# Attention in a two-layer hybrid backbone: the value products of a pair of heads in one group, six buffers of transposed probabilities for four

## The chip, the cores and the metric

One core of a Trainium2 chip runs the whole program. The metric is the device time of one execution in microseconds (us); lower is better. TensorE is PE in the rows (its weight loads are PEld), VectorE is DVE, ScalarE is ACT, GpSimd is POOL, and SP issues the DMAs.

## What is computed

The reference is a backbone of two layers (DEPTH = 2) over 1024 latent and 256 context tokens, 1024 wide, in float32. A layer is a normalised input projection whose columns go to four mixers (mLSTM, differential attention, GLA, gated DeltaNet), a concatenation and an output projection. Only the attention is touched. It has 4 heads of width 64; each head has two maps of queries and keys of width 32:

```python
s = jnp.einsum('bhjqd,bhjkd->bhjqk', qblk, k).astype(F32) * scale
p = jax.nn.softmax(s, axis=-1)
wts = p[:, :, 0] - lam * p[:, :, 1]
return jnp.einsum('bhqk,bhkd->bhqd', wts.astype(v.dtype), v)
```

A block of 128 latent queries reads 1280 keys, a block of context queries 256. The second layer computes no context queries.

## The kernel before, in words

**How the order of the work is made.** The program is written as strands, Python functions that run as coroutines while the kernel is built. A planner (class `Issue`, line 141) keeps a modelled time for each engine and picks, for every instruction, the strand that can start earliest by that model; between strands that could start at the same time the lower rank goes first (`choose`, line 256). A strand whose instruction has waited over 3 us of modelled time (`patience`, line 143) goes ahead of all ranks. `need` stops a strand until another has issued the work of that name, `set` says that it was issued. On the chip each engine then runs its instructions in the order in which they were picked, with semaphores for the data.

**The strands of a layer.** The strand `left` (line 1180) does the input projection (rank 4, tile `mm`), then mLSTM, and asks for the end of the attention before mLSTM is opened (line 1189). The strand `right` (line 1200) does gated DeltaNet, then the attention, then GLA. So projection matmuls of rank 4 fill TensorE during the attention, and again during GLA until the projection is done.

**The attention (line 2276).** An item is one head and one block of 128 queries; a pair `m` is the two heads of one feature half for the same block, items 2m and 2m+1. There are 20 pairs in the first layer, 16 of them with 1280 keys (10 tiles of 128) and 4 with 256, and 16 pairs with 1280 keys in the second. The strands count cycles `c`, one item to a cycle:

- `on_pe` (line 2431, rank 0) issues the scores of item c: for map 0 two products of 512 columns into `sc0`, then both maps' 256 context keys into `sc2`, then map 1 into `sc1`. Each of these PSUM tiles has one buffer, so the next item's scores wait for the exponentials of this item.
- `on_dve` (line 2510, rank 0) takes the maxima, and one cycle later combines the two maps' probabilities in place (`p<-p,st,p`).
- `on_act` (line 2467, rank 0) takes the exponentials of each map, first of the 256 context keys, then of the 1024 latent keys. Between them it copies transposed probabilities from PSUM to SBUF (`turned`, line 2383, tile `wt`).
- `on_pe2` (line 2444, rank 1) transposes the combined probabilities (`turn`, line 2367, tile `tr`, one PSUM buffer), multiplies them with the values (`values`, line 2397, tile `po`, one PSUM buffer), and transposes the result back (`back`, line 2418).

The 10 key tiles of a pair are transposed in six steps k = 0 to 5: step k takes head k % 2 and the tiles 4(k // 2) onwards, so 4, 4, 4, 4, 2 and 2 tiles. A step's transposes wait for the ScalarE copy of the step before. `values(m, g)` is the group g of four tiles for both heads: two matmuls per tile, one on either half of the array's columns, 16, 16 and 8 matmuls for g = 0, 1, 2. Group 0 opens the tile `po`, and waits for `ev("A", m - 1)`, VectorE's reading of the pair before (`aacc`).

For pair m the cycles are 2m+3, 2m+4 and 2m+5. The order on TensorE in an odd cycle, where pair m starts and pair m-1 ends, is: step 0 of m; group 2 of m-1; step 1 of m; back of m-1; step 2 of m; group 0 of m. In the even cycle after it: step 3, step 4, group 1, step 5, all of m.

The copies on ScalarE have fixed places: steps 1 and 4 between the small and the large exponential of map 0, steps 2 and 5 after that large one, and the next cycle's step 0 or 3 at the end of the cycle; after step 0 of pair m+1 follows the copy `ot` of pair m's result.

Of the kernel before, what the change touches and what calls it, by code (L numbers as in the profile page):

```python
# [35 lines left out]
GRP = ((0, 2), (2, 4), (6, 4))  # L36
# [393 lines left out]
def _build(tc, nc, A, out, root, dbg):  # L430
    q_ = Issue()
    q_.log = dbg.get("log")
    V, S, G, P = (Eng(q_, e, r) for e, r in zip("VSGP", (nc.vector, nc.scalar, nc.gpsimd, nc.tensor)))
# [32 lines left out]
    def mark(label):  # L466
        if q_.me:
            q_.me.label = label
# [68 lines left out]
    with ExitStack() as st:  # L537
        ps = Pool(st, "crps", PSUM)([128, 512], "tr")[:, :16]
# [1737 lines left out]
    def attention(L):  # L2276
# [5 lines left out]
        with ExitStack() as st:  # L2282
            ap_ = Pool(st, "att", side="right")
            pps = Pool(st, "atps", PSUM, "right")
            KT = {}
            vt = ap_([128, NT, 256], "av")
# [41 lines left out]
            for f, t in [(f, t) for f in range(2) for t in L.yt]:  # L2328
                acc = Box()
                for h in (2 * f, 2 * f + 1):  # L2330
                    it = Box()
# [12 lines left out]
            def ev(*k):  # L2344
                return (l, "att", *k)
# [21 lines left out]
            def turn(m, k):  # L2367

                it, c0 = items[2 * m + k % 2], 4 * (k // 2)
                c = min(4, it.nk - c0)  # L2370
                if c <= 0:
                    return
                q_.need(ev("C", 2 * m + k % 2))
                if seq:
                    q_.need(ev("cp", *seq[-1]))
                seq.append((m, k))
                pt = pps([128, 512], "tr")
                for i in range(c):
                    P.transpose(pt[:, 128 * i:128 * i + 128], it.p[0][:, 128 * (c0 + i):128 * (c0 + i) + 128], ident)
                D["pt", m, k] = pt, c  # L2380
                q_.set(ev("T", m, k))

            def turned(m, k):
                if items[2 * m].nk <= 4 * (k // 2):
                    return
                q_.need(ev("T", m, k))
                i = seq.index((m, k))
                if i > 3:
                    m_, k_ = seq[i - 4]
                    q_.need(ev("V", m_, k_ // 2))  # L2390
                pt, c = D.pop(("pt", m, k))
                wt = ap_([128, 4, 128], "wt", 4)
                S.copy(wt[:, :c, :], pt[:, :128 * c].rearrange("p (a b) -> p a b", b=128))
                D["wt", m, k] = wt
                q_.set(ev("cp", m, k))

            def values(m, g):

                pair = items[2 * m:2 * m + 2]
                nk = pair[0].nk  # L2400
                if nk <= 4 * g:
                    return
                q_.need(ev("cp", m, 2 * g), ev("cp", m, 2 * g + 1))
                if g == 0:
                    if m:
                        q_.need(ev("A", m - 1))
                    D["po", m] = pps([128, 256], "po")
                po = D["po", m]
                for i in range(4 * g, min(4 * g + 4, nk)):
                    gr, c = pair[0].tiles[i]  # L2410
                    for x, it in enumerate(pair):
                        P.matmul(po[64 * x:64 * x + 64, 0:128], vt[:, GRP[gr][0] + c, 64 * it.h:64 * it.h + 64], D["wt", m, 2 * g + x][:, i % 4, :],
                                 start=(i == 0), stop=(i == nk - 1), tile_position=(0, 64 * x))
                q_.set(ev("V", m, g))
                if 4 * g + 4 >= nk:
                    q_.set(ev("V", m))

            def back(m):
                q_.need(ev("o", m))
                P.transpose(D["po", m][:, 128:256], D["ot", m], ident)  # L2420
                q_.set(ev("B", m))

            D, seq = {}, []
# [3 lines left out]
            def pairs(c):  # L2427

                return [(m, c - 2 * m - 3) for m in range(NP_) if 0 <= c - 2 * m - 3 <= 2]
# [14 lines left out]
            def on_pe2():  # L2444
                mark(f"{l}att.T")
                for c in CY:
                    ps = dict((a, m) for m, a in pairs(c))
                    if 0 in ps:
                        turn(ps[0], 0)
                    if 1 in ps:  # L2450
                        turn(ps[1], 3)
                    if 2 in ps:
                        values(ps[2], 2)
                    if 0 in ps:
                        turn(ps[0], 1)
                    if 1 in ps:
                        turn(ps[1], 4)
                        values(ps[1], 1)
                    if 2 in ps:
                        back(ps[2])  # L2460
                    if 0 in ps:
                        turn(ps[0], 2)
                        values(ps[0], 0)
                    if 1 in ps:
                        turn(ps[1], 5)

            def on_act():
                mark(f"{l}att.S")
                for c in CY:
# [9 lines left out]
                    for j in range(2):  # L2479
                        if c < n:  # L2480
                            it = items[c]
                            o = 128 * it.nk - 256
                            q_.need(ev("m", c, j))
                            S.activation(it.p[j][:, o:o + 256], it.small[:, j, :], AF.Exp, bias=it.st[:, j:j + 1],
                                         accum_out=it.st[:, 4 + j:5 + j])
                            q_.set(ev("e", c, j))
                        if j == 0:
                            for x in (0, 1):
                                if x in a:
                                    turned(a[x], (1, 4)[x])  # L2490
                        if c < n:
                            if full[c]:
                                S.activation(it.p[j][:, 0:1024], it.big[j], AF.Exp, bias=it.st[:, j:j + 1],
                                             accum_out=it.st[:, 6 + j:7 + j])
                            q_.set(ev("E", c, j))
                        if j == 0:
                            for x in (0, 1):
                                if x in a:
                                    turned(a[x], (2, 5)[x])
                    for x in (0, 1):  # L2500
                        if x in b:
                            turned(b[x], (0, 3)[x])
# [81 lines left out]
            q_.spawn(0, sums)  # L2584
            q_.spawn(RANK["att norm"], norms)
            q_.spawn(RANK["att pe"], on_pe2)
            on_pe()
            q_.need(ev())
# [352 lines left out]
```

## Time and profile before

| | |
|---|---|
| time, median of 3 runs | 2445.36 us (2436.24 to 2446.64) |
| the profiled execution's own time | 2444.86 us |
| its span in the trace | 2443.0 us |
| busy: PE, PEld, DVE, ACT, POOL | 88%, 72%, 62%, 40%, 35% of the span |
| attention, first and last value product, first layer | 662.3 us, 899.4 us |
| attention, first and last value product, second layer | 1923.4 us, 2121.6 us |
| value matmuls (`po<-wt,av`) | 1312, 103.0 us busy |
| transposes of probabilities (`tr<-k_ident,p`) | 656, 114.7 us busy |

The shares of the whole span mix stages with different limits. The attention is read from a stretch of it, in the order of time, engine by engine. In such a view a row gives the start, the duration, the engine, the operation with its written and read tiles, the sizes, the number of instructions merged, and in brackets the idle time before it with what ended that idle time.

### The profile page before, as it was taken

What the parts mean: (1) busy time and instruction counts of PE and PEld (TensorE: products, weight loads), DVE (VectorE), ACT (ScalarE), POOL (GpSimd) and SP (SyncE); (2) the same over time, 40 slices, a digit from 0 to 9 for tenths busy, and PEclk for the clock granted to TensorE, in tenths of its full rate; (3) what the DMA queues carried; (4) which work ended last, traced back from release to release, by engine and by line L of the source; (5) the groups of instructions that cost most, each with busy time, mean ns of one, the idle gap of its engine ahead of it and who ended that gap; (6) DMA issues with size and microseconds to landing.
All of it is one profiled execution on the core that took longest, in us unless ns stands there. A gap on an engine that the chain in (4) does not pass through costs nothing.

```text
span 2443.0 us, 57689 instructions
## 1 busy us (share of the span) xinstructions
PE 2141.1 (88%) x23367; PEld 1762.3 (72%) x23367; DVE 1513.1 (62%) x2676; ACT 987.4 (40%) x2169; POOL 850.4 (35%) x1075
## 2 busy tenths in 40 slices
PE   5899999999898998886868798889999989977888
PEld 1656778888776687865756677888888667866776
DVE  3586679555386854546556396686642778555665
ACT  2346412333376853222424255412322677533240
POOL 1343523554122225241522163623442122254340
PEclk8899999999999999988989899999999999976989
DMA  7347643455513134157953135432444331353694
GB/s 260 116 133 228 198 140 109 138 152 157 143 46 91 51 84 147 51 143 213 279 178 133 43 124 173 158 113 93 148 149 126 91 100 38 75 152 85 186 277 172
DMA packets 348051, 335.37 MB, mean 137 GB/s; under 512 B 93146, under 2 KB 292282, under 8 KB 347274
## 3 DMA queue, kind: packets, MB, share of 16 engines
q1 hardware_dynamic: 347786, 331.69, 45.6%
q8 instruction: 185, 3.03, 0.5%
q14 instruction: 80, 0.66, 0.1%
HBM read 226.78 MB, written 107.43 MB: 137 GB/s over the span
## 4 chain that ended last, share of the span: by engine, by line
PE 55%; DMA 13%; DVE 11%; issue 8%; ACT 6%; SPq 5%; POOL 2%; ACTq 0%; POOLq 0%; DVEq 0%
PE mm L406 26%; PE po L406 5%; SPq L406 5%; PE tr L406 4%; PE o L406 4%; PE sc L406 3%; PE p L406 3%; PE pd L406 3%; DVE st L406 2%; DMA wm<-in_w_mod 2%; PE puw L406 2%; ACT p L406 2%; PE m L406 2%; DVE cacc L406 1%; DMA KT<-akh 1%
## 5 line engine op out<-in xcount | busy, mean ns | idle before, releaser
L406 PE MATMUL mm<-w,hT 128*128 128x256 f32 x4512 | 645.6, 294 | 20.7 <-DVE st L406 10.0
L406 PEld LDWEIGHTS mm<-w,hT 128*128 128x128 f32 x4512 | 580.9, 195 | 52.9 <-issue 20.4
L406 PE MATMUL mm<-hT,w 128*128 128x512 f32 (+1 forms) x1680 | 388.9, 377 | 19.0 <-DVE w L406 4.9
L406 PEld LDWEIGHTS mm<-hT,w 128*128 128x128 f32 x1680 | 283.1, 195 | 90.0 <-issue 19.6
L406 DVE TENSOR_REDUCE st<-sc 128x1 f32<-128x1024 f32 (+1 forms) x200 | 200.2, 1027 | 69.8 <-PE sc L406 68.3
L406 ACT ACTIVATE p<-sc,st 128x256 f32<-128x256 f32 (+1 forms) x272 | 211.3, 786 | 68.8 <-DVE st L406 54.8
L406 POOL TENSOR_TENSOR w<-wr,w 128x512 fp32r<-128x512 f32 x62 | 87.4, 1411 | 235.5 <-ACT w L406 199.4
L406 POOL TENSOR_TENSOR hss<-hss,mhalf 128x2 f32<-128x2 f32 (+2 forms) x72 | 105.7, 1467 | 181.7 <-DVE hss L406 175.8
L406 PE MATMUL o<-wo,yT 128*128 128x512 f32 x540 | 155.2, 425 | 8.6 <-DVE x L406 7.1
L406 PE MATMUL sc<-KT,qt 96*128 96x512 f32 (+1 forms) x400 | 124.9, 402 | 30.3 <-DMA KT<-akh 13.3
L406 POOL TENSOR_TENSOR ss<-ss,mhalf 128x1 f32<-128x1 f32 (+1 forms) x39 | 68.2, 1749 | 193.4 <-DVE ss L406 185.4
L406 PEld LDWEIGHTS o<-wo,yT 128*128 128x128 f32 x540 | 105.7, 202 | 34.7 <-issue 5.6
L406 ACT COPY st<-mm 128x512 f32<-128x512 f32 (+1 forms) x83 | 45.8, 552 | 202.0 <-PE mm L406 140.9
L406 ACT COPY wt<-tr 128x512 f32<-128x512 f32 (+1 forms) x200 | 102.2, 511 | 60.4 <-PE tr L406 59.8
L406 PE MATMUL o<-w,yT 128*128 128x512 f32 x324 | 107.3, 462 | 21.8 <-DVE st L406 12.3
L406 PE MATMUL tr<-k_ident,p 128*128 128x128 f32 x656 | 114.7, 280 | 7.5 <-ACT wt L406 7.2
L406 POOL TENSOR_TENSOR st<-st 128x1 f32<-128x1 f32 (+1 forms) x136 | 26.6, 195 | 266.5 <-ACT p L406 196.9
L406 ACT CAST w<-wr 128x512 fp32r<-128x512 f32 x128 | 76.8, 620 | 103.7 <-PE mm L406 52.6
L406 PEld LDWEIGHTS sc<-KT,qt 96*128 96x128 f32 x400 | 63.8, 197 | 60.4 <-ACT p L406 32.0
L406 PE MATMUL po<-wt,av 128*64 128x128 f32 x1312 | 103.0, 282 | 2.0 <-DVE aacc L406 2.0
L406 DVE SCALAR_TENSOR_TENSOR p<-p,st,p 128x1280 f32<-128x1280 f32 (+1 forms) x72 | 103.0, 1431 | 2.6 <-POOL st L406 2.5
L406 DVE TENSOR_TENSOR w<-wr,w 128x512 fp32r<-128x512 f32 x66 | 59.1, 895 | 68.6 <-ACT w L406 64.9
(315 smaller groups left out, 4125.8 us busy)
## 6 DMA issues: line engine op xcount, KB each, us to landing
wr<-in_w_in SPq DMA_DIRECT2D x64, 512.0 KB
wm<-in_w_mod SPq DMA_DIRECT2D x64, 256.0 KB
y<-y SPq DMA_DIRECT2D x36, 256.0 KB
xp<-st SPq DMA_DIRECT2D x18, 512.0 KB
pd<-rs_NG SPq DMA_DIRECT2D x18, 512.0 KB
kq<-kq SPq DMA_DIRECT2D x18, 512.0 KB
x<-xp SPq DMA_DIRECT2D x18, 512.0 KB
wm<-in_w_mod SPq DMA_DIRECT2D x16, 512.0 KB
```

The costliest lines, as they stand in the source:

```text
L406: r = fn(*a, **k)
```

## The change

`values` loses its argument g and issues all the products of a pair at once, 40 for 10 key tiles, after all six copies. It is called at the start of the odd cycle 2m+5, ahead of step 0 of the next pair. The tile `wt` has six buffers for four, and a copy asks for the whole pair's products that read its buffer's last contents, not for one group's.

```diff
@@ turned @@
-                if i > 3:
-                    m_, k_ = seq[i - 4]
-                    q_.need(ev("V", m_, k_ // 2))
+                if i > 5:
+                    q_.need(ev("V", seq[i - 6][0]))
...
-                wt = ap_([128, 4, 128], "wt", 4)
+                wt = ap_([128, 4, 128], "wt", 6)
@@ values @@
-            def values(m, g):
+            def values(m):
...
-                if nk <= 4 * g:
-                    return
-                q_.need(ev("cp", m, 2 * g), ev("cp", m, 2 * g + 1))
-                if g == 0:
-                    if m:
-                        q_.need(ev("A", m - 1))
-                    D["po", m] = pps([128, 256], "po")
-                po = D["po", m]
-                for i in range(4 * g, min(4 * g + 4, nk)):
+                q_.need(*(ev("cp", m, k) for k in range(6) if nk > 4 * (k // 2)))
+                if m:
+                    q_.need(ev("A", m - 1))
+                po = D["po", m] = pps([128, 256], "po")
+                for i in range(nk):
...
-                q_.set(ev("V", m, g))
-                if 4 * g + 4 >= nk:
-                    q_.set(ev("V", m))
+                q_.set(ev("V", m))
@@ on_pe2 @@
                     ps = dict((a, m) for m, a in pairs(c))
+                    if 2 in ps:
+                        values(ps[2])
                     if 0 in ps:
                         turn(ps[0], 0)
                     if 1 in ps:
                         turn(ps[1], 3)
-                    if 2 in ps:
-                        values(ps[2], 2)
                     if 0 in ps:
                         turn(ps[0], 1)
                     if 1 in ps:
                         turn(ps[1], 4)
-                        values(ps[1], 1)
                     if 2 in ps:
                         back(ps[2])
                     if 0 in ps:
                         turn(ps[0], 2)
-                        values(ps[0], 0)
                     if 1 in ps:
                         turn(ps[1], 5)
```

## Rows read from the trace of the kernel before

**Rows 1.** The page's head and its part 1: busy us, share of the span, instructions.

```profile
span 2443.0 us, 57689 instructions
...
PE 2141.1 (88%) x23367; PEld 1762.3 (72%) x23367; DVE 1513.1 (62%) x2676; ACT 987.4 (40%) x2169; POOL 850.4 (35%) x1075
```

**Rows 2.** Windows of both attentions: PE, PEld, DVE, ACT, POOL busy, PEclk, DMA share, GB/s.

```profile
660.00:925.00 265.00, 242.34 (x1992) 193.55 (x1991) 194.63 (x368) 178.38 (x458) 71.11 (x159) 0.97 0.29 77
1890.00:2125.00 235.00, 213.69 (x1639) 168.82 (x1639) 180.81 (x315) 163.64 (x406) 56.83 (x133) 0.96 0.27 73
```

**Rows 3.** Timeline of 712 to 726 us, TensorE: one pair's period.

```profile
712.32 0.39 PE L406 MATMUL tr<-k_ident,p 128*128 128x128 f32 x2
...
712.63 1.09 PE L406 MATMUL po<-wt,av 128*64 128x128 f32 x16
...
713.67 0.44 PE L406 MATMUL tr<-k_ident,p 128*128 128x128 f32 x2
...
714.77 0.72 PE L406 MATMUL sc<-KT,qt 96*128 96x512 f32 x2
...
715.34 0.38 PE L406 MATMUL tr<-k_ident,p 128*128 128x128 f32 x2
...
715.50 0.51 PE L406 MATMUL sc<-KT,qt 96*128 96x256 f32 x2
...
715.85 0.38 PE L406 MATMUL tr<-k_ident,p 128*128 128x128 f32 x2
...
716.16 0.66 PE L406 MATMUL po<-wt,av 128*64 128x128 f32 x8
...
716.75 0.39 PE L406 MATMUL mm<-w,hT 128*128 128x256 f32 x1
...
721.25 1.09 PE L406 MATMUL po<-wt,av 128*64 128x128 f32 x14
...
722.26 0.73 PE L406 MATMUL sc<-KT,qt 96*128 96x512 f32 x2
...
722.93 0.43 PE L406 MATMUL po<-wt,av 128*64 128x128 f32 x2
...
723.29 0.66 PE L406 MATMUL tr<-k_ident,p 128*128 128x128 f32 x4
...
725.04 1.09 PE L406 MATMUL po<-wt,av 128*64 128x128 f32 x16
```

**Rows 4.** The same timeline, ScalarE and VectorE.

```profile
712.79 0.48 ACT L406 ACTIVATE p<-sc,st 128x256 f32<-128x256 f32 x1 [0.58 <-PE tr L406]
...
714.61 0.38 ACT L406 COPY wt<-tr 128x256 f32<-128x256 f32 x1
...
715.54 1.82 DVE L406 TENSOR_REDUCE st<-sc 128x1 f32<-128x1024 f32 x2 [1.16 <-PE sc L406]
...
716.40 0.62 ACT L406 COPY wt<-tr 128x512 f32<-128x512 f32 x1
...
716.87 0.32 ACT L406 COPY ot<-po 128x128 f32<-128x128 f32 x1
...
717.65 0.48 ACT L406 ACTIVATE p<-sc,st 128x256 f32<-128x256 f32 x1 [0.46 <-DVE st L406]
...
720.44 0.47 DVE L406 TENSOR_SCALAR aacc<-po,st 128x64 f32<-128x64 f32 x2
...
724.04 0.59 ACT L406 COPY wt<-tr 128x512 f32<-128x512 f32 x1 [1.50 <-PE tr L406]
```

**Rows 5.** Windows with the projection's tile mm alone: PE, PEld, DVE, ACT busy.

```profile
1020.00:1040.00 20.00, 14.44 (x118) 13.83 (x117) 1.32 (x2) 1.20 (x2) 1.00 0.21 55
1040.00:1060.00 20.00, 0.52 (x4) 0.31 (x3) 0.68 (x1) 0.60 (x1) 0.83 0.55 148
...
2160.00:2180.00 20.00, 11.10 (x72) 9.56 (x71) 0.68 (x1) 0.96 (x2) 0.93 0.32 95
2180.00:2200.00 20.00, 0.00 (x0) 0.00 (x0) 0.69 (x1) 0.22 (x1) 0.59 0.38 64
```

More of the change, by code (lines that the diff above doesn't have):

```diff
@@ L2395, in turned @@
                 q_.set(ev("cp", m, k))
-            def values(m, g):
+            def values(m):
                 pair = items[2 * m:2 * m + 2]
                 nk = pair[0].nk
-                if nk <= 4 * g:
-                    return
-                q_.need(ev("cp", m, 2 * g), ev("cp", m, 2 * g + 1))
-                if g == 0:
-                    if m:
-                        q_.need(ev("A", m - 1))
-                    D["po", m] = pps([128, 256], "po")
-                po = D["po", m]
-                for i in range(4 * g, min(4 * g + 4, nk)):
+                q_.need(*(ev("cp", m, k) for k in range(6) if nk > 4 * (k // 2)))
[3 more added lines that the diff above has]
+                for i in range(nk):
                     gr, c = pair[0].tiles[i]
                     for x, it in enumerate(pair):
-                        P.matmul(po[64 * x:64 * x + 64, 0:128], vt[:, GRP[gr][0] + c, 64 * it.h:64 * it.h + 64], D["wt", m, 2 * g + x][:, i % 4, :],
+                        P.matmul(po[64 * x:64 * x + 64, 0:128], vt[:, GRP[gr][0] + c, 64 * it.h:64 * it.h + 64], D["wt", m, 2 * (i // 4) + x][:, i % 4, :],
                                  start=(i == 0), stop=(i == nk - 1), tile_position=(0, 64 * x))
-                q_.set(ev("V", m, g))
-                if 4 * g + 4 >= nk:
-                    q_.set(ev("V", m))
+                q_.set(ev("V", m))
             def back(m):
```

## The prediction, made before the changed kernel ran

> **What bounds the kernel now.** I read the page's shares first, then windows of the two attentions, then one pair of heads in the order of time, and last the windows that tell when the projection ends. Over the whole span TensorE is busy 88% [rows 1], but that is a mean over many stages, so it says only that no other engine comes near. In the two attentions TensorE is busy 242.34 us of 265 and 213.69 of 235, 91% both times, with VectorE at 73 to 77% and ScalarE at 67 to 70% [rows 2]. The granted clock there is 0.97 and 0.96, nearly always the upper level, so it has nothing to give.
>
> One pair's period is 12.41 us: the same run of 16 value products starts at 712.63 and again at 725.04 [rows 3]. Within it the reader should see four runs of value products on TensorE, of 16, 8, 14 and 2: group 1 and group 2 of one pair, and group 0 of the next, which the scores at 722.26 cut in two. ScalarE, which has the exponentials, waits for TensorE twice in that period: 1.50 us before the copy of step 3 at 724.04, and 0.58 us before the small exponential at 712.79 (the same wait comes back one period later, at 725.20) [rows 4]. The first wait is the loop to look at. Group 0 cannot start before VectorE has read the pair before (`aacc` from 720.44), so its first 14 products start at 721.25, the scores and 2 more products follow, and only then, at 723.29, come the transposes of step 3 that ScalarE is waiting for [rows 3, 4].
>
> The projection, which fills TensorE's gaps, is not done when the attention is: its last matmuls fall in 1040 to 1060 and in 2160 to 2180 [rows 5], some 140 us and 50 us after the attentions' last value products.
>
> **The change, part by part.** (a) **Fewer runs of value products.** The run of 16 takes 1.04 us up to the next instruction (712.63 to 713.67), that of 8 takes 0.59, that of 14 takes 1.01, that of 2 takes 0.36 [rows 3]. From 2 to 14 that is 0.65 us for 12 products, 0.055 us each, so 0.15 us of a run's time is not products. On the way in, two transposes take 0.31 us up to a run (712.32 to 712.63) and 0.16 up to scores (715.34 to 715.50) [rows 3]: another 0.15. A run costs 0.3 us of TensorE beyond its products. The products themselves are the same 40. With one run for four a pair saves 0.9 us of TensorE, 29 us over 32 long pairs; with no run fewer it saves nothing.
>
> The Trainium skill bears on this run cost (TensorEngine Tiling (Array Packing), Key Properties): it says that changing the tiling mode, as opposed to the tile, drains TensorE. The trace's 0.3 us agrees with a drain on either side; the page has no figure, and by its rule alone the sum would be the 29 us gained.
>
> I take about three runs, not one. The strand that issues the group has rank 1 and the scores have rank 0, and by line 340 the planner holds each product for 0.11 us, so 40 of them for 4.4 us. Within that time the scores of the small keys and of map 1 of the running item come free and are put in. That saves 0.3 us of a pair.
>
> (b) **The wait that goes.** Step 3 no longer stands behind group 0, nor behind `aacc`. ScalarE's 1.50 us and the 0.58 us that follow from it go [rows 4]. What then limits the way from the odd item's small exponential to the next even item's is the ordinary loop of scores, maxima and exponentials. The trace has that loop once without the wait: from the even item's small exponential at 712.79 to the odd item's at 717.65, 4.86 us, with 0.46 us of it waiting for VectorE [rows 4]. Today the other half takes 12.41 - 4.86 = 7.55 us. I take 4.9 to 5.1 for it afterwards.
>
> (c) **The wait that comes.** All 40 products now stand ahead of step 0 of the next pair, and ScalarE has the copy of step 0 in its own order at 716.40, in front of `ot` and of the odd item's exponentials [rows 4]. The products need the copy of step 5, which starts at 714.61 and takes 0.38. The scores at 714.77 hold TensorE until 715.34, where today the transposes of step 0 start at once [rows 3]. So: 715.34, plus 40 products at 0.055 (2.2 us), plus three runs at 0.3 (0.9), plus the two sets of scores that cut in, at most 0.35 (715.50 to 715.85) and 0.57 (714.77 to 715.34), 0.9 together: 719.3. From a step's transposes to its copy is 0.75 us (723.29 to 724.04), which makes 720.1, 3.7 us later than today. The copy and `ot` take until 717.19 today, 0.8 us; the odd item's small exponential then starts at 720.9 and not at 717.65. The even half becomes 720.9 - 712.79 = 8.1 us, the odd half about 5.0, the period 13.1. I take 13.0, since today's 0.57 for scores includes their way into transposes: **0.6 us more for a pair**.
>
> The ends: a group that nothing cuts ends at 715.34 + 2.2 + 0.3 = 717.8, the exponential starts at 719.4, and the period is 6.6 + 4.9 = 11.5, 0.9 us less than now. With five runs (the filler of rank 4 also gets in after 3 us of waiting) it is 0.6 us more than in the sum above, up to 13.7, 1.3 us more than now. The two halves meet today's period when the block from 715.34 takes 3.4 us (12.41 - 5.0 = 7.4, so an exponential at 720.2 and transposes at 718.7).
>
> (d) **Six buffers** remove no wait of their own: no row of the period shows ScalarE stopped by a `wt` buffer, and the products of pair m are issued ahead of step 0 of pair m+1 in any case. They are needed because the group reads all six. No DMA is added or moved.
>
> (e) **The sum.** Of the 32 long pairs about 26 run in the steady pattern; I leave out three for each layer, where the pipeline fills and empties. 26 x 0.6 = 16 us more of attention, 8 for each layer. Not all of it arrives. TensorE goes on with projection matmuls during the added time, and the projection, which mLSTM waits for, ends well behind the attention [rows 5]; what starts later is GLA, on the other strand. I let a third arrive, because GLA and mLSTM share the engines afterwards: 5 us. None and all of it are the ends. At the end of each attention the last group is 40 products instead of 8, 32 x 0.055 = 1.8 us, beside projection work; I count it at nothing, and at 3.6 us if that cover is gone. The profiled execution took 2444.86 us, 1.9 more than its span [rows 1] and 0.5 less than the median. I add the 5 us to the median: **2450 us**.
>
> **The rivals.** *Faster, by runs.* The planner leaves the group nearly whole. The period falls by up to 0.9 us, 26 x 0.9 = 23 us, or TensorE's 29 us go to the projection, which then ends earlier. For it speaks that TensorE is 91% busy [rows 2]; against it that scores cut group 0 in two already today, at 722.26 [rows 3]. About 2420 us. The point is the 3.4 us block of (c).
>
> *Slower, by the copy of step 0.* The place is ScalarE's copy at 716.40, now behind the whole block, and behind it `ot` and the odd item's exponentials. Cut into five runs the block costs 1.3 us for a pair, 34 us over 26 pairs; it decides once the block is longer than 3.4 us and GLA's later start is no longer covered. With three quarters of it arriving: 2445 + 25 = 2470 us. For it speaks that TensorE has hardly a gap in the period; against it the projection that fills the added time [rows 5].
>
> *No such change.* The planner cuts the group as often as today, and places the filler so that step 0 comes in time; or its other order elsewhere moves the time by as much as the attention does. About 2445 us.
>
> **How the numbers follow.** A measurement of this kernel can tell about 0.5%, 12 us, from no change. The forecast (2450, its own range 2438 to 2457) has a chance of 0.33 and "no such change" 0.10, both within 0.5%: 0.43. Faster by runs, 0.27. Slower by step 0, 0.30. I let the range run from 2420, the first rival's time, to 2474, just beyond the second's: a third of the first rival and a third of the second stay outside, about 2 in 10.
>
> **What would show it.** Right: the row of step 3's copy has no wait on TensorE; the copy of step 0 has one of some 3 us; the value products come in three or so runs a pair, between them scores; a period near 13.0; the projection's last matmul no later than now, GLA's start some 8 us later per layer. Wrong: a period under 12.4 with the 40 products in one run (then the first rival holds), or a wait at step 0 under 2 us. If the period grows by over 1 us and the projection also ends later, the second rival holds.

## The result, and the profile of the changed kernel

The change makes the kernel slower: 2477.95 us (median of 4 runs, 2461.04 to 2479.35) against 2444.89 us, a ratio of 1.0122 with a 95% interval of 1.0093 to 1.0151. That is 33 us. The forecast of 2450 us is missed, and the measured time lies 4 us above the range. The profiled execution took 2476.63 us.

The page's head and its part 1 answer to [rows 1]:

```profile
span 2474.8 us, 57689 instructions
...
PE 2154.2 (87%) x23367; PEld 1773.9 (72%) x23367; DVE 1509.4 (61%) x2679; ACT 987.4 (40%) x2178; POOL 831.1 (34%) x1065
```

The work is the same, and ScalarE's busy time has not moved at all. TensorE's is 13 us more: the value products alone (group `po<-wt,av`), which the change was to make cheaper, are busy 110.7 us for 103.0. Where time goes is told by the groups of the page's part 5 (busy us, mean ns, then idle time of the engine before the group, and what ended most of it). First two lines of before, then the same two of after:

```profile
L406 DVE TENSOR_REDUCE st<-sc 128x1 f32<-128x1024 f32 (+1 forms) x200 | 200.2, 1027 | 69.8 <-PE sc L406 68.3
...
L406 ACT COPY wt<-tr 128x512 f32<-128x512 f32 (+1 forms) x200 | 102.2, 511 | 60.4 <-PE tr L406 59.8
```

```profile
L406 DVE TENSOR_REDUCE st<-sc 128x1 f32<-128x1024 f32 (+1 forms) x200 | 199.8, 1023 | 87.2 <-PE sc L406 86.6
...
L406 ACT COPY wt<-tr 128x512 f32<-128x512 f32 (+1 forms) x200 | 103.1, 515 | 123.4 <-PE tr L406 123.4
```

ScalarE's copies wait for their transposes 123.4 us and not 59.8. The wait was to vanish at step 3, and there it did: the mean idle time before that copy, over the 16 long pairs of a layer, fell from 1.48 and 1.29 us (first and second layer) to 0.09 and 0.05. Before the copy of step 0 it rose from 0.19 and 0.05 us to 3.10 and 3.12. The median period of a pair went from 12.33 to 13.68 us in the first layer and from 12.41 to 14.0 in the second.

One block of the second attention shows how, TensorE and ScalarE in the order of time; it answers to [rows 3, 4]:

```profile
2069.04 0.95 PE L406 MATMUL mm<-w,hT 128*128 128x256 f32 x6
...
2069.78 0.38 ACT L406 COPY wt<-tr 128x256 f32<-128x256 f32 x1
2069.92 0.43 PE L406 MATMUL po<-wt,av 128*64 128x128 f32 x2
...
2070.28 0.96 PE L406 MATMUL sc<-KT,qt 96*128 96x512 f32 x4
...
2071.18 1.09 PE L406 MATMUL po<-wt,av 128*64 128x128 f32 x14
...
2072.20 0.73 PE L406 MATMUL sc<-KT,qt 96*128 96x512 f32 x2
...
2072.86 0.87 PE L406 MATMUL po<-wt,av 128*64 128x128 f32 x10
...
2073.66 0.38 PE L406 MATMUL mm<-w,hT 128*128 128x256 f32 x1
2073.97 1.09 PE L406 MATMUL po<-wt,av 128*64 128x128 f32 x14
...
2074.99 0.66 PE L406 MATMUL tr<-k_ident,p 128*128 128x128 f32 x4
...
2075.74 0.58 ACT L406 COPY wt<-tr 128x512 f32<-128x512 f32 x1 [4.02 <-PE tr L406]
```

The reader should see that the 40 products still come in four runs (2, 14, 10, 14), and that everything which cuts them stands ahead of step 0's transposes. Over all long pairs the mean is 3.3 runs in the first layer and 3.7 in the second; before, it was 3.7 in both. From 2069.92 to 2074.99 the block takes 5.07 us: 3.20 of it are the four runs, 1.56 two sets of scores (2070.28 to 2071.18 and 2072.20 to 2072.86), 0.31 one projection matmul. Behind it ScalarE's copy has waited 4.02 us. The block is a usual one: its median is 4.87 us in the first layer and 4.88 in the second.

What fills the longer period is the projection. These are windows of its tile `mm` alone (PE busy and matmuls first), before and then after, each with the first layer's attention, the stretch from 1360 to the second attention, the second attention, and what follows it:

```profile
652.00:900.00 248.00, 98.03 (x505) 73.56 (x506) 3.42 (x5) 6.27 (x11) 0.97 0.25 70
...
1360.00:1898.00 538.00, 370.91 (x2249) 317.04 (x2249) 20.00 (x30) 32.03 (x57) 0.97 0.42 128
1898.00:2122.00 224.00, 82.00 (x416) 61.78 (x417) 4.10 (x6) 5.47 (x9) 0.96 0.25 69
2122.00:2200.00 78.00, 44.49 (x324) 42.04 (x324) 2.71 (x4) 4.14 (x7) 0.83 0.58 147
```

```profile
651.00:915.00 264.00, 113.40 (x627) 86.84 (x628) 5.17 (x8) 7.15 (x12) 0.97 0.24 70
...
1360.00:1915.00 555.00, 385.60 (x2330) 329.12 (x2330) 22.91 (x34) 30.67 (x55) 0.96 0.40 125
1915.00:2165.00 250.00, 104.23 (x558) 80.86 (x559) 4.11 (x6) 7.41 (x12) 0.95 0.25 71
2165.00:2200.00 35.00, 12.38 (x102) 11.92 (x100) 2.06 (x3) 1.77 (x3) 0.73 0.73 182
```

From its first scores to its last value product the attention takes 263.7 us for 247.4 in the first layer (+16) and 248.9 for 223.5 in the second (+25). Of that, 15.4 us (113.40 less 98.03) and 22.2 us (104.23 less 82.00) are projection matmuls that used to run later. So the added time is not lost to TensorE. Nor is the clock a rival here: the granted clock of these attentions is 0.97 and 0.95, for 0.97 and 0.96 before. Whether it costs anything depends on what ends last behind the attention. The windows that answer to [rows 5]:

```profile
1020.00:1040.00 20.00, 13.00 (x95) 11.55 (x94) 1.33 (x2) 1.19 (x2) 1.00 0.09 29
1040.00:1060.00 20.00, 0.00 (x0) 0.00 (x0) 0.67 (x1) 0.00 (x0) 0.69 0.66 166
2160.00:2180.00 20.00, 15.11 (x119) 14.11 (x117) 1.38 (x2) 1.77 (x3) 1.00 0.67 116
2180.00:2200.00 20.00, 0.00 (x0) 0.00 (x0) 0.68 (x1) 0.00 (x0) 0.52 0.64 211
```

The projection ends no later in either layer: at 1038.7 for 1040.2 us, and at 2178.5 for 2179.1. GLA's first small products (tile `pd`) start 18.8 us later in the first layer (920.7 to 939.5) and 35.7 later in the second (2165.0 to 2200.7). In the first layer the last of them comes at 1023.6 us (1008.3 before), still ahead of the projection's end, and the second layer's first projection matmul starts at 1281.0 us for 1283.4. In the second layer the row below, of before and then of after (tile `pd`, first and last start), shows GLA ending behind the projection already before the change:

```profile
L406 PE MATMUL pd<-qm,km x3456: 184/194/259, 920.7 to 2223.8; 32*32 32x32 f32 x192
```

```profile
L406 PE MATMUL pd<-qm,km x3456: 184/209/258, 939.5 to 2257.7; 32*32 32x32 f32 x192
```

2223.8 lies 45 us after 2179.1. In both traces the chain that ended last goes through GLA's products up to the last of them, and from there into the output projection (tile `o`). So GLA's delay of 33.9 us (2257.7 less 2223.8) arrives at the end: the span grew by 31.8. Of that delay 17.1 us are there already when the second attention starts (1915.3 for 1898.2), and the attention adds 25.4. The way from its last value product to GLA's last product is 8.7 us shorter (93.5 for 102.2), with 102 projection matmuls left behind the attention for 324.

### The profile page after: what moved, and what is told of

It reads as the page before. It is cut to its first block, busy times and chain, and to the rows that moved or that the text cites. A ratio compares the mean times of both kernels' runs of the same rounds, so it can differ in the third digit from the quotient of the medians.

```text
span 2474.8 us, 57689 instructions
## 1 busy us (share of the span) xinstructions
PE 2154.2 (87%) x23367; PEld 1773.9 (72%) x23367; DVE 1509.4 (61%) x2679; ACT 987.4 (40%) x2178; POOL 831.1 (34%) x1065
## 5 line engine op out<-in xcount | busy, mean ns | idle before, releaser
L406 PE MATMUL mm<-w,hT 128*128 128x256 f32 x4512 | 654.0, 294 | 22.2 <-DVE st L406 11.7
L406 DVE TENSOR_REDUCE st<-sc 128x1 f32<-128x1024 f32 (+1 forms) x200 | 199.8, 1023 | 87.2 <-PE sc L406 86.6
L406 ACT ACTIVATE p<-sc,st 128x256 f32<-128x256 f32 (+1 forms) x272 | 212.4, 792 | 50.3 <-DVE st L406 31.7
L406 POOL TENSOR_TENSOR hss<-hss,mhalf 128x2 f32<-128x2 f32 (+2 forms) x72 | 97.9, 1359 | 179.1 <-DVE hss L406 173.2
L406 ACT COPY wt<-tr 128x512 f32<-128x512 f32 (+1 forms) x200 | 103.1, 515 | 123.4 <-PE tr L406 123.4
L406 PE MATMUL tr<-k_ident,p 128*128 128x128 f32 x656 | 111.5, 281 | 24.7 <-ACT wt L406 24.4
L406 PE MATMUL po<-wt,av 128*64 128x128 f32 x1312 | 110.7, 289 | 0.3 <-DVE aacc L406 0.3
L406 PEld LDWEIGHTS tr<-k_ident,p 128*128 128x128 f32 x656 | 72.5, 141 | 51.1 <-ACT wt L406 42.5
L406 DVE SCALAR_TENSOR_TENSOR p<-p,st,p 128x1280 f32<-128x1280 f32 (+1 forms) x72 | 102.9, 1430 | 2.5 <-POOL st L406 2.2
L406 PEld LDWEIGHTS po<-wt,av 128*64 128x64 f32 x1312 | 81.8, 142 | 27.0 <-issue 17.2
```

What stands on the lines that cost most here:

```text
L406: r = fn(*a, **k)
```

## The experiments

Ratios are to the kernel before, measured beside each. The period is the median over the long pairs of the first and the second layer; the attention is the time from the first scores to the last value product, in each layer of one trace. The last two columns are the page's sums of ScalarE's copies waiting for transposes and of VectorE's maxima waiting for scores.

| kernel | ratio, 95% interval | period, us | attention, us | copies wait | maxima wait |
|---|---|---|---|---|---|
| before | | 12.33, 12.41 | 247.4, 223.5 | 59.8 | 68.3 |
| after | 1.0122 (1.0093 to 1.0151) | 13.68, 14.0 | 263.7, 248.9 | 123.4 | 86.6 |
| first layer only | 1.0029 (1.0011 to 1.0047) | 13.69, 12.45 | 264.8, 225.5 | 92.5 | 76.2 |
| second layer only | 1.0106 (1.0083 to 1.0128) | 12.33, 14.01 | 247.3, 244.8 | 90.3 | 78.9 |
| before, six buffers | 1.0012 (0.9997 to 1.0027) | 12.33, 12.46 | 247.0, 227.5 | 62.5 | 74.2 |
| after, modelled product 0.055 | 1.0068 (1.0045 to 1.0092) | 13.79, 13.97 | 261.4, 243.2 | 111.5 | 99.8 |
| before, modelled product 0.055 | 1.0018 (1.0002 to 1.0033) | 12.13, 12.15 | 245.9, 225.8 | 56.4 | 69.8 |
| after, group uncut | 1.0085 (1.0067 to 1.0103) | 13.22, 13.11 | 271.2, 246.6 | 60.7 | 102.9 |
| after, step 0 ahead of the group | 1.0062 (1.0039 to 1.0085) | 13.10, 13.26 | 260.4, 237.7 | 89.7 | 56.5 |
| group 0 right after step 3 | 0.9966 (0.9952 to 0.998) | 11.12, 11.18 | 227.0, 209.9 | 17.6 | 52.9 |
| two groups, 32 and 8 | 0.9912 (0.989 to 0.9934) | 10.63, 11.26 | 229.5, 212.4 | 32.9 | 52.1 |
| two groups, modelled product 0.055 | 0.9964 (0.9947 to 0.9981) | 11.45, 11.40 | 239.1, 220.5 | 39.6 | 69.7 |

Where the time arrives is read from stretches of one trace each, in us: up to the second layer's first projection matmul; from there to the second attention's first scores; that attention; from its last value product to the end of the last instruction.

| kernel | up to layer 2 | to its attention | its attention | behind it |
|---|---|---|---|---|
| before | 1283.4 | 614.7 | 223.5 | 317.3 |
| before, six buffers | 1290.6 | 616.9 | 227.5 | 313.4 |
| after | 1281.0 | 634.3 | 248.9 | 306.8 |
| first layer only | 1279.1 | 634.4 | 225.5 | 305.9 |
| second layer only | 1290.0 | 617.1 | 244.8 | 319.7 |
| after, group uncut | 1268.0 | 639.3 | 246.6 | 307.2 |
| group 0 right after step 3 | 1271.5 | 631.5 | 209.9 | 321.8 |
| two groups, 32 and 8 | 1255.4 | 637.2 | 212.4 | 311.0 |

The first two rows have the same order of instructions and so show what such lengths are worth: 7 us in the first column, 2 to 4 in the others. In the whole change the first layer is no longer than before, and all of the loss lies in the second: some 18 us ahead of its attention, 21 to 25 in it, and 7 to 10 regained behind it.

**The change in the first layer only.** The old groups are kept beside the new one, and the layer chooses.

```diff
+            one = l == 0
...
-                wt = ap_([128, 4, 128], "wt", 4)
+                nb = 6 if one else 4
+                wt = ap_([128, 4, 128], "wt", nb)
...
+                    if one and 2 in ps:
+                        values(ps[2])
```

> The change in the first layer alone. Theory (the first layer's longer attention is covered, because the projection that mLSTM waits for ends well behind it and GLA's delay is made up before the layer ends): the first attention is 16 us longer, as in the changed kernel, the projection's last matmul stays within 3 us of 1040 us, and the whole time is 2440 to 2452 us. Rival A (half of each layer's lengthening arrives): about 2460 us. Rival B (the planner, starting from other modelled times, puts the second layer's projection into an order that costs about 15 us before the second attention): the second attention's first scores start near 1915 us instead of 1898, and the whole is about 2460 us.

Measured: 1.0029. The first attention takes 264.8 us, as long as in the whole change, but the second layer begins no later (1279.1 us): of the 16 us nothing is to be seen there. What does arrive, about 7 us, comes from somewhere the edit doesn't touch, as the expectation's rival B had it. From the first attention on the planner makes another order, and it puts 1536 and 710 matmuls of the projection's two forms between 1300 us and the second attention for 1469 and 696 (15 us of TensorE by the windows of `mm` above, where the whole change has the same counts). The stretch ahead of that attention is 634.4 us for 614.7 to 617.1 in the three traces with the old order, the attention keeps its old period of 12.45 us, and behind it 8 to 11 us are regained. The counts alone do not explain that stretch: the uncut group below has 1469 and 696 again and takes 639.3 us. Which part of the order makes it longer stays open.

**The change in the second layer only.** The same with `one = l == 1`.

> The change in the second layer alone. Theory (there GLA's end decides, so the longer attention arrives whole): scores start at 1898 us as before, the attention is 25 us longer, GLA's first small product is 25 to 30 us later, and the whole time is 2468 to 2475 us. Rival A (half arrives): about 2457 us. Rival B (the lengthening is covered here too, and the changed kernel lost its time ahead of the second attention): 2440 to 2452 us.

Measured: 1.0106, 26 us. The order is that of before up to the second attention (1469 and 696 matmuls again), the attention takes 244.8 us for 223.5 (227.5 with six buffers, in the same order), the wait before step 0 is 3.20 us and before step 3 0.04. GLA's last `pd` moves from 2223.8 to 2246.5; since it stands at 2237.6 in the trace with six buffers, that shift alone proves little. By the timed ratios the second layer brings most of the loss, and 7 + 26 us of the two halves make the whole change's 33.

**Six buffers alone.**

```diff
-                if i > 3:
-                    m_, k_ = seq[i - 4]
+                if i > 5:
+                    m_, k_ = seq[i - 6]
...
-                wt = ap_([128, 4, 128], "wt", 4)
+                wt = ap_([128, 4, 128], "wt", 6)
```

> The kernel before with six buffers of transposed probabilities and nothing else. The order of TensorE's and ScalarE's instructions is that of before. By the prediction's step (d) no wait is removed: ratio 0.998 to 1.002, period 12.4 us, the wait of step 3 still 1.2 to 1.5 us. If the buffers held something back, the period falls below 12.2 us and the ratio below 0.998.

Measured: 1.0012, with 1 inside the interval; period 12.46 us in the second layer, the wait at step 3 1.38. The buffers neither cost nor bring anything. This run also shows how far single traces can be trusted: with the same order its second attention ended at 2134.9 us, 13 us later than in the trace of before, 9 of them there when it started. A shift of that size between two traces proves nothing by itself; the argument rests on lengths within one trace, on counts of instructions and on timed ratios.

**What the planner believes of a value product.** It models 0.11 us for each; the trace gives 0.055.

```diff
+            elif n == 128 and m == 64 and rows == 128:
+                dur = 0.055
```

Once in the changed kernel, and once in the kernel before:

> The changed kernel, with the planner's modelled time of a value product at 0.055 us instead of 0.11, the time that the trace shows. Theory (the planner holds the group for twice its time, so scores and filler cut into it and more filler is put around it): 3 runs of value products for a long pair instead of 4, 25 to 30 projection matmuls in a pair instead of 37, a period of 13.2 us instead of 14.0, and 2450 to 2462 us. Rival (the cuts come from scores that are free by then in any case, and the filler does not hold the chain): 4 runs, a period of 14 us, 2470 to 2480 us.

> The kernel before, with the planner's modelled time of a value product at 0.055 us instead of 0.11. Theory (with groups of 16 and 8 the planner's error changes little): period 12.2 to 12.5 us, 2436 to 2452 us. Rival (the error costs the kernel before as well, through filler placed for longer gaps than there are): 2420 to 2434 us.

Measured: 1.0068 and 1.0018. In the changed kernel the group is still cut (typically 2, 2, 20, 16, or 28, 2, 10; 2.9 runs a pair), the period stays at 13.8 and 14.0 us and the wait before step 0 at 2.9: the rival's period, with the time at the upper end of the theory's. The modelled length of a product is therefore only a small part of why the block is long. The two attentions are 8 us shorter together than in the changed kernel, and the ratio says 13; the rest was gained elsewhere, in stages whose order changed with it. In the kernel before, the cut of group 0 goes in most pairs (16, 16, 8) and the period falls by 0.20 and 0.26 us: close to the 0.3 us that the prediction's step (a) gave for one run. The time does not follow; again 1536 projection matmuls for 1469 stand ahead of the second attention, and the stretch up to it is 633.5 us.

**The group never cut.** The strand of the transposes gets a rank ahead of the scores.

```diff
-         "att pe": 1,
+         "att pe": -0.5,
```

> The changed kernel, with the strand of transposes and value products ranked ahead of the scores, so that a group stays in one run. Theory (the length of the block ahead of step 0 makes the period): the block from the copy of step 5 to the transposes of step 0 falls from 5 us to about 3, ScalarE's wait at step 0 from 4.0 us to under 2.5, the period to 12.4 to 12.8 us, and the whole to 2440 to 2455 us. Rival (the scores, put off until the group is done, hold VectorE's maxima instead): ScalarE's wait moves from the copy of step 0 to the exponentials, the period stays at 13.7 to 14.2 us, the whole at 2470 to 2480 us.

Measured: 1.0085. The timeline of one block, TensorE, ScalarE and VectorE:

```profile
2044.96 2.40 PE L406 MATMUL po<-wt,av 128*64 128x128 f32 x40
...
2047.30 0.66 PE L406 MATMUL tr<-k_ident,p 128*128 128x128 f32 x4
2047.71 0.48 PE L406 MATMUL sc<-KT,qt 96*128 96x512 f32 x1
...
2048.05 0.59 ACT L406 COPY wt<-tr 128x512 f32<-128x512 f32 x1 [1.18 <-PE tr L406]
...
2048.58 1.82 DVE L406 TENSOR_REDUCE st<-sc 128x1 f32<-128x1024 f32 x2 [1.86 <-PE sc L406]
```

Forty products in one run take 2.34 us up to the next instruction (2044.96 to 2047.30). Step 0's copy waits 1.18 us here, but now the scores stand behind the group, and VectorE's maxima wait 1.86. In the trace all 32 long pairs have one run. In the sums, the copies' wait is back at 60.7 us, the level of before, and the maxima's has gone from 68.3 to 102.9. The rival "faster by runs" had the block it asked for, 2.34 us where 3.4 was its point, and was slower all the same: a group of 40 ahead of the next pair holds up either the copy or the scores. Neither expectation came out whole: the wait moved as the rival had it, and the period lies between the two. The attentions are not shorter than in the changed kernel (271.2 and 246.6 us), but there the clock takes part: the granted clock is 0.92 and 0.93 in them, so this run does not price the uncut group alone.

```profile
L406 DVE TENSOR_REDUCE st<-sc 128x1 f32<-128x1024 f32 (+1 forms) x200 | 199.6, 1022 | 103.0 <-PE sc L406 102.9
...
L406 ACT COPY wt<-tr 128x512 f32<-128x512 f32 (+1 forms) x200 | 102.8, 514 | 61.1 <-PE tr L406 60.7
```

**Step 0 ahead of the group.** One of the two things behind the group is taken from there.

```diff
+                    if 0 in ps:
+                        turn(ps[0], 0)
                     if 2 in ps:
                         values(ps[2])
-                    if 0 in ps:
-                        turn(ps[0], 0)
...
-                wt = ap_([128, 4, 128], "wt", 6)
+                wt = ap_([128, 4, 128], "wt", 7)
```

The copy `ot` moves behind the copy of step 1, and a seventh buffer takes the copy of step 0.

> The changed kernel with the transposes of step 0 put ahead of the group, the result's copy moved behind step 1, and seven buffers. Theory (what ScalarE has in its own order behind the group sets the period): the wait moves from the copy of step 0 to that of step 1 and falls from 3.1 us to about 1.8, since one copy and a small exponential now lie beside the group; the period falls from 14 to 13.0 to 13.3 us, the time to 2455 to 2466 us. Rival (the scores and maxima behind a long group set it, wherever the group stands): the period stays at 13.7 to 14.2 us, 2470 to 2480 us.

Measured: 1.0062, period 13.10 and 13.26 us. In the second layer the mean wait before step 0 falls to 0.35 us, all but 0.03 of it in the last pair, and before step 1 it is 2.13: the next copy in ScalarE's order takes the wait over.

```profile
2035.92 1.96 PE L406 MATMUL po<-wt,av 128*64 128x128 f32 x30
...
2037.82 0.65 PE L406 MATMUL tr<-k_ident,p 128*128 128x128 f32 x4
...
2038.56 0.59 ACT L406 COPY wt<-tr 128x512 f32<-128x512 f32 x1 [2.04 <-PE tr L406]
```

**Group 0 right after step 3.** If a large group late in the cycle is the harm, a small group out of step 3's way should be the gain. From the kernel before, with six buffers:

```diff
                     if 1 in ps:
                         turn(ps[1], 3)
+                        values(ps[1], 0)
...
                         turn(ps[0], 2)
-                        values(ps[0], 0)
```

> The kernel before with six buffers and one call moved: group 0 of a pair is issued after the transposes of its step 3, ahead of step 1 of the next pair; groups 1 and 2 stay where they are. So step 3 no longer stands behind group 0, but the value products still come in three groups, three or four runs a pair. Two groups (32 and 8) gave 0.991 with a period of 10.6 to 11.3 us. Theory A, the place: what that kernel gained was the wait of step 3 (1.3 to 1.5 us a pair) and no copy made later by more than one group of 16. Then this one has under 0.4 us of wait at step 3, a period of 11.2 to 11.8 us and a ratio of 0.991 to 0.996. Theory B, the runs: it gained by two runs of value products for four, 0.6 us of TensorE a pair. Then this one has a period of 12.0 us or more and a ratio of 0.997 to 1.001.

Measured: 0.9966, period 11.12 and 11.18 us, close to theory A. The place alone is enough for that: with the value products still in four runs (typically 12, 4, 16, 8; 3.8 a pair) the period falls by 1.2 us, and in the second layer no step's mean wait is above 0.26. The attentions take 227.0 and 209.9 us, the shortest of all kernels here. The ratio is smaller than that gain: the stretch ahead of the second attention is 631.5 us in this order, and the second layer as a whole no shorter than before.

**Two groups, 32 and 8.** Groups 0 and 1 together, after step 4, when step 3's copy and VectorE's reading of the pair before are both done; six buffers.

```diff
                     if 1 in ps:
                         turn(ps[1], 4)
+                        values(ps[1], 0)
                         values(ps[1], 1)
...
                         turn(ps[0], 2)
-                        values(ps[0], 0)
```

> The kernel before with six buffers, and groups 0 and 1 issued together behind step 4, group 2 where it was. Theory (ScalarE waits where a block stands ahead of a copy with too little work between): the wait at step 3 goes, a wait of 0.8 to 1.5 us comes at step 5, none at step 0, the period is 11.8 to 12.3 us and the time 2430 to 2446 us, no slower than the kernel before. Rival (any block of over 2 us costs as in the changed kernel, through the scores or the copies): period over 13 us, 2455 to 2475 us.

Measured: 0.9912, 2424.61 us for 2445.82: faster than both kernels, and faster than the expectation, as the wait at step 5 is 0.6 us in the mean and not 0.8 to 1.5. The page's part 1 and the group of copies:

```profile
PE 2122.6 (88%) x23367; PEld 1760.1 (73%) x23367; DVE 1520.1 (63%) x2683; ACT 992.8 (41%) x2173; POOL 844.6 (35%) x1068
...
L406 ACT COPY wt<-tr 128x512 f32<-128x512 f32 (+1 forms) x200 | 102.6, 513 | 34.3 <-PE tr L406 32.9
```

The period is 10.63 and 11.26 us. A block of its timeline:

```profile
2014.16 1.97 PE L406 MATMUL po<-wt,av 128*64 128x128 f32 x32
...
2016.06 0.44 PE L406 MATMUL tr<-k_ident,p 128*128 128x128 f32 x2
...
2016.31 0.73 PE L406 MATMUL sc<-KT,qt 96*128 96x512 f32 x2
...
2016.59 0.37 ACT L406 COPY wt<-tr 128x256 f32<-128x256 f32 x1 [0.33 <-PE tr L406]
```

The run of 32 stands ahead of step 5, whose copy comes late in ScalarE's order, behind a large exponential: it waits 0.33 us. With 2.1 runs a pair for 3.7, the value products are busy 90.8 us for 103.0. TensorE as a whole is busy 18.5 us less than before (2141.1 in [rows 1]), but that is not the price of the runs: the next kernel has as few runs, 91.8 us of value products, and 2139.9 us of TensorE. Beside the kernel with group 0 after step 3 the attentions are 2.5 us longer each, so the 13 us between the two kernels do not lie there. In the first attention 478 projection matmuls find room for 422, the projection of that layer ends at 1028.8 us for 1051.8, and the second layer begins at 1255.4 for 1271.5. That fits TensorE's time saved by fewer runs, but it was not separated from the other order of the stages. Against the kernel before, all of the gain lies ahead of the second layer: this one takes 1160.6 us, and 1155.5 and 1157.8 in the two traces of before's order, although its attention is 11 to 15 us shorter.

**Two groups, with the modelled product of 0.055 us.**

> The kernel of two groups, with the planner's modelled time of a value product at 0.055 us. Theory (a block that the planner knows at its true length gets less cut and less filler ahead of step 5): period 11.7 to 12.1 us, 2420 to 2440 us. Rival (the order elsewhere, planned from other times, moves the whole by more than the attention does): a shorter attention, and a time of 2445 to 2460 us.

Measured: 0.9964, period 11.45 and 11.40 us. A truer figure for one instruction does not make the planner's whole order better.

## Why the prediction was wrong

**(a) Runs.** The price held for a whole run: a run of 40 should take 40 x 0.055 + 0.15 = 2.35 us up to the next instruction, and took 2.34. The 0.15 comes from the runs of 16 and 8, though; those of 2 and 14, from which the 0.055 was taken, leave 0.25. A run of 2 costs as much as a run of 4, so a cut costs more than the prediction had it. The count failed: "about three runs" was argued from the modelled 0.11 us, and 3.3 and 3.7 came in the mean, with a projection matmul among them besides the scores. The 0.3 us a pair were not saved: the value products' busy time rose by 7.7 us. With half the modelled time the group was still cut into 2.9 runs, so the modelled time is not the main reason for the cuts.

The Trainium skill (TensorEngine Tiling (Array Packing), Key Properties) says that a change of tiling mode drains TensorE. The traces agree that a run has a cost of its own: 40 products took 2.34 us in one run and 3.20 in four, with what stood between them left out. That this cost is a drain no run here shows. The step that the rule leaves out is that the cost is paid in TensorE time, while the attention here is paced by whoever waits behind a run.

**(b) The wait at step 3** went, as said. The odd to even half was to be 4.9 to 5.1 us and is 5.81 (small exponentials at 2062.15 and 2067.96; the medians are 5.58 and 5.81). The prediction took the even to odd half's 4.86 for it, and two things differ. Between the small and the large exponential ScalarE has step 1's copy of four tiles here (0.59 us at 2062.90) and step 4's of two there (0.36 at 713.25), so the large exponential starts 1.23 us after the small one for 0.71, and the next scores 0.5 us later. And VectorE reads the scores that start at 2064.65 only at 2065.78, 1.13 us later for 0.77 before: in front of the maxima stand a weight split for the projection and the `aacc` of the late pair, which before fell elsewhere.

```profile
2062.90 0.59 ACT L406 COPY wt<-tr 128x512 f32<-128x512 f32 x1 [0.17 <-PE tr L406]
...
2063.38 1.12 ACT L406 ACTIVATE p<-sc,st 128x1024 f32<-128x1024 f32 x1
...
2064.51 0.95 DVE L406 TENSOR_TENSOR w<-wr,w 128x512 fp32r<-128x512 f32 x1
2064.65 0.74 PE L406 MATMUL sc<-KT,qt 96*128 96x512 f32 x2
...
2065.39 0.47 DVE L406 TENSOR_SCALAR aacc<-po,st 128x64 f32<-128x64 f32 x2
...
2065.78 1.81 DVE L406 TENSOR_REDUCE st<-sc 128x1 f32<-128x1024 f32 x2
```

**(c) The wait at step 0** came where it was placed, and the 0.75 us from transposes to copy are exact (2074.99 to 2075.74). The block was forecast at 4.0 us (715.34 to 719.3) and takes 5.07: scores of 1.56 us for 0.9, 0.31 of projection not counted, and 3.20 for the runs where 3.1 was counted. So it was mostly the scores that were mis-sized. The even to odd half is 8.42 us (2067.96 to 2076.38; the medians are 7.90 and 8.22) for 8.1. Both halves together give 14.2 for 13.1; a pair costs 1.3 us more (41.6 us of attention over 32 pairs), the second rival's price, and not 0.6.

**(d) Six buffers** held: 1.0012 alone.

**(e) What arrives** is the step that failed in kind. "I let a third arrive" spread one share over two layers that differ. [Rows 5] say that the projection ends behind the attention in both, and that is true; but the delayed strand goes on through GLA, and the row to look for was GLA's last product against the projection's last: 1008.3 against 1040.2 in the first layer, 2223.8 against 2179.1 in the second. So the first layer's 16 us vanished and the second's came whole: its attention is 17 to 25 us longer, and the second layer's change alone cost 26 by the timed ratio. With that and the measured period the sum would have been 2445 + 25 = 2470, the second rival's figure; that the two agree is partly luck, since the rival let three quarters of both layers arrive. The other 7 us are the planner's other order of a stage that the change doesn't touch, which the prediction named as a rival's part, but not as an addition. The rule of the two ends is argued from these traces and not the whole story of the first layer: with group 0 right after step 3 the projection ends later there (1051.8 us), and the second layer still begins 12 us earlier.

The second rival, slower by the copy of step 0, had place and price right. Its sign, that the projection would also end later, was wrong: it ended at 2178.5. The first rival fell with the uncut group, as far as a run at a lower clock can show it. Its point of 3.4 us looked at the copy alone and not at the scores, which must stand on one side of the group or the other.

## What to carry to other kernels

On engines that run in a fixed order, grouping work saves what a run costs and delays everything queued behind the group by its whole length; list who stands behind it on that engine, and put the group ahead of the consumer whose turn comes last. Here the kernel with 40 products ahead of the next pair was 1.2% slower, and the one with 32 of them ahead of step 5 was 0.9% faster. To price a later end of a stage, find for each layer the strand that ends last behind it: in the first layer here the filler moved ahead and hid the delay, in the second it was not what the next stage waited for. And compare whole stretches: a stage that the planner reorders can take back what the attention gained.

## What the runs showed of the hardware

Two executions of one order of instructions (before, and before with six buffers) stood 13 us apart late in the trace (2121.6 and 2134.9 for the last value product), though the timed ratio was 1.0012; a shift between two single traces is worth less than a length within one. By the starts of the instructions behind them, runs of these value products go in steps of four: the medians, each over one trace, are 0.36 us for 2 products and 0.37 for 4, 0.58 and 0.59 for 6 and 8, 1.02 for 14, 1.02 to 1.04 for 16, 1.90 for 32 and 2.34 for 40; the run of 30 above took 1.90 as well. That is 0.15 us and 0.22 for each four begun, so a cut inside a four costs more than one between two.
